# A down projection by seven products of 2x2 blocks, and the last modulation columns in the up loop

## The chip, the cores and the metric

The kernel runs on one core of a Trainium2 chip. Five engines work side by side on a common on-chip memory of 128 partitions (SBUF): TensorE (PE in the profile; PEld is its load of the stationary operand), VectorE (DVE), ScalarE (ACT), GpSimd (POOL) and SyncE (SP), which here only issues DMAs. TensorE writes to PSUM, eight banks of 128 x 512 fp32. Each engine works through its own instructions in order and waits on semaphores for the others. The metric is the device time of one execution in microseconds, the median of several runs.

## The reference

One layer of a diffusion backbone, for a prompt of 128 tokens and a sample of 512, both of width 1024. What matters here is the second half of the layer, a ConvFFN with a gain `g2` that comes from a conditioning vector, and the norm at the end:

```python
mod = jax.nn.silu(cvec) @ lw['w_ada'] + lw['b_ada']
sh1, sc1, g1, sh2, sc2, g2 = jnp.split(mod, 6, axis=-1)
...
h = rmsnorm(x, lw['norm2_g']) * (1.0 + sc2) + sh2
x = x + g2 * conv_ffn(h, lw['w_up'], lw['ffn_conv_w'], lw['ffn_conv_b'], lw['w_down'])
...
def conv_ffn(h, w_up, cw, cb, w_down):
    z = dwconv3(h @ w_up, cw, cb)
    a, g = jnp.split(z, 2, axis=-1)
    return (jax.nn.silu(g) * a) @ w_down
...
y_sample = rmsnorm(xs, final_norm_g)
```

`w_up` is 1024 x 5632, `w_down` 2816 x 1024, all in fp32.

## The kernel before

The 640 tokens (four tiles of 128 of the sample, one of the prompt) go through the layer together. Every fp32 product is made of three matmuls on two-part operands: the high part is a rounded copy made by ACT (`act(..., AF.Copy)`), the low part the difference, made by DVE (`tensor_tensor(..., subtract)`); high x high, high x low and low x high are added up in PSUM.

**The up loop** (`up_all`, `up_pair`, lines 1503 to 1657) runs over 22 pairs of an a-tile and a g-tile of the 2816 hidden features. Each pair is a product of 2x2 blocks with seven multiplications (`prod`, 12 matmuls of 320 columns each) in place of eight. The order of every engine is written out by hand there: calls through `ovec`, `opool` and `oact` keep their program order while `fixed[0]` is set. In `up_pair(p_)` TensorE works on pair p_ and on the last two products of pair q = p_ - 1; DVE makes the low parts and block sums of the weights of pair n = p_ + 1 (`up_al`, `up_sums`, `up_bl`), moves products out of PSUM (`first_sum` and the subtractions into `ubuf`), and runs the three-tap convolution of the pairs q and o = p_ - 2 (`taps`, two instructions of 128x641) and the gate (`gated`); ACT makes high parts, copies products and does `centre` and `gate`. POOL issues DMAs: two that make low parts by adding in memory (`low_dma`), and `keep`, which writes the finished 128x641 tile of activations to `actd` in DRAM. The tiles X1 (`xz`), X0 and MG1 (`ubuf`) hold the loop's intermediates, G half of the raw weights, F the block sums.

**The down stage** (`down_prep`, `down_tile`, `down_out`, lines 1695 to 1779) runs over two halves of the 1024 output columns and, in each, over 11 pairs of hidden tiles. A unit is one pair in one half: five token tiles x two hidden tiles x three matmuls of 512 columns with the activations stationary. Its operands are prepared two units ahead: 128x1024 of weights, and two activation tiles of 128x640 that are read back from `actd` in groups. The last three units of the second half are held, and their matmuls run token tile by token tile, each followed by its output steps. Tile's scheduler chooses the order within an engine here, by program order and readiness. Beside it `ada_cols` (lines 231 to 270) computes the columns 40 to 47 of the modulation, which are `g2`: a load of 128x1024 of `w_ada`, and for each of the two conditioning vectors one DVE instruction that multiplies and sums along the row. The finished columns are transposed on TensorE and go through DRAM (`gain_rows`) to be broadcast to all partitions (`gain_load`, into S0). The residual stream `x2` comes back from DRAM to X0, X1 and G (`x2r`) during the stage.

DMAs of weights are issued by SP, in program order: one that waits for its target to come free holds back those behind it. The tiles with tags `w`, `raw` and `gt` have 3, 3 and 4 buffers, those made by `region` one each.

## Time and profile before

| what | value |
|---|---|
| median of 3 runs | 1036.48 us (1036.42 to 1037.4) |
| the profiled execution | 1039.72 us, its span 1038.0 us, granted clock 0.994 |
| up loop, pairs 4 to 21 | 12.32 us a pair |
| last matmul of the up loop | 884.4 us after the span's start |
| down stage, a unit of 30 matmuls | 6.80 us |

An execution's own time is a little longer than its span in the trace, and the profiled one is a little longer than the median; times read in the trace are microseconds from the span's start. In rows of the trace `out<-in` names the tiles that an instruction writes and reads, `x12` is a count, a bracket tells how long the engine was idle before and what it waited for, and L146 is the line of the helper that records the hand-ordered calls, so there the tiles tell the instructions apart.

### The profile page before, as it was taken

How to read it: one execution, taken by the hardware profiler on the slowest of the kernel's cores; microseconds unless marked ns; L12 is line 12 of the kernel's file. 1: busy time of each engine (PE TensorE's matmuls, PEld its weight loads, DVE VectorE, ACT ScalarE, POOL GpSimd, SP SyncE). 2: the span in 40 equal slices, each digit the busy share in tenths (PEclk: the TensorE clock that was granted, in tenths of full speed). 3: DMA queues.
4: the chain of work that ended last, by engine and by line, in shares of the span. 5: the costliest groups of instructions: out<-in, count | busy, mean ns of one | idle time of the engine just before them, and what ended most of it. 6: DMA issues, size and time to landing. Idle time of an engine off the chain costs nothing.

```text
span 1038.0 us, 18800 instructions
## 1 busy us (share of the span) xinstructions
PE 1022.1 (98%) x7644; PEld 963.4 (93%) x7644; DVE 790.9 (76%) x1287; ACT 523.4 (50%) x905; POOL 95.8 (9%) x139
## 2 busy tenths in 40 slices
PE   8999999999999999999999999999999999999997
PEld 6899989998999999999998889999999999888886
DVE  6758889789956567767768689998888887795734
ACT  6642343342333444444445377876677776632532
POOL 1000010201100000000000021211111121000201
PEclk9999989999999999999999999999999999999998
DMA  9864433454144132332268385666655569974212
GB/s 355 317 212 131 126 96 122 131 179 152 52 141 140 52 102 81 124 102 77 66 229 328 132 260 144 173 168 166 163 149 151 148 152 260 373 250 156 82 41 102
DMA packets 54295, 165.68 MB, mean 160 GB/s; under 512 B 7968, under 2 KB 14912, under 8 KB 52160
## 3 DMA queue, kind: packets, MB, share of 16 engines
q1 hardware_dynamic: 44432, 137.19, 39.1%
q0 software_dynamic: 9776, 27.28, 11.3%
q8 instruction: 60, 0.98, 0.4%
q14 instruction: 27, 0.22, 0.1%
HBM read 131.52 MB, written 21.52 MB: 147 GB/s over the span
## 4 chain that ended last, share of the span: by engine, by line
PE 96%; DMA 2%; DVE 1%; issue 1%; ACT 0%; SPq 0%; POOL 0%; POOLq 0%
PE g L352 20%; PE g L1430 20%; PE m L1089 14%; PE g L1745 8%; PE m L1745 6%; PE m L1430 5%; PE g L1102 4%; PE m L1225 3%; PE g L901 2%; PE g L1225 2%; PE m L146 2%; PE g L146 1%; PE m L513 1%; DMA A<-in_w_ada_dram 1%; PE m L838 1%; PE m L801 1%
## 5 line engine op out<-in xcount | busy, mean ns | idle before, releaser
L352 PE MATMUL g<-XH,w 128*128 128x320 f32 x832 | 201.1, 319 | 0.0
L352 PEld LDWEIGHTS g<-XH,w 128*128 128x128 f32 x832 | 143.7, 191 | 2.0 <-issue 1.2
L352 PE MATMUL g<-XL,w 128*128 128x320 f32 x416 | 130.0, 312 | 0.0
L352 PEld LDWEIGHTS g<-XL,w 128*128 128x128 f32 x416 | 79.3, 191 | 0.3 <-issue 0.2
L304 DVE TENSOR_TENSOR w<-raw,w 128x1024 fp32r<-128x1024 f32 x34 | 41.6, 1222 | 18.8 <-ACT w L303 18.1
L1745 PE MATMUL g<-w,XH 128*128 128x512 f32 (+1 forms) x216 | 47.5, 372 | 0.0
L303 ACT ACTIVATE w<-raw 128x1024 fp32r<-128x1024 f32 x34 | 35.8, 1052 | 21.1 <-PE g L1225 10.2
L1745 PEld LDWEIGHTS g<-w,XH 128*128 128x128 f32 x216 | 38.5, 188 | 7.5 <-ACT XH L1708 0.3
L1089 PE MATMUL m<-XH,w 128*128 128x320 f32 x192 | 45.0, 309 | 0.0
L146 DVE SCALAR_TENSOR_TENSOR X<-MG,p2t,X 128x641 f32<-128x641 f32 x44 | 38.9, 885 | 5.7 <-ACT X L146 4.8
L316 ACT ACTIVATE w<-raw 128x1024 fp32r<-128x1024 f32 (+1 forms) x26 | 29.4, 1130 | 24.7 <-PE g L352 11.9
L146 DVE SCALAR_TENSOR_TENSOR X<-X,p2t,X 128x641 f32<-128x641 f32 x44 | 38.9, 885 | 2.0 <-ACT X L146 1.0
L1745 PE MATMUL m<-w,XH 128*128 128x512 f32 (+1 forms) x180 | 40.2, 368 | 0.0
L1745 PE MATMUL g<-w,XL 128*128 128x512 f32 (+1 forms) x180 | 40.1, 373 | 0.0
L1430 PE MATMUL g<-XL,C 128*128 128x320 f32 x240 | 38.6, 310 | 0.4 <-ACT MG L146 0.4
L1430 PE MATMUL g<-XL,w 128*128 128x320 f32 x240 | 38.7, 310 | 0.0
L317 DVE TENSOR_TENSOR w<-raw,w 128x1024 fp32r<-128x1024 f32 (+1 forms) x26 | 33.9, 1304 | 6.1 <-ACT w L316 5.8
L1745 PEld LDWEIGHTS g<-w,XL 128*128 128x128 f32 x180 | 32.2, 188 | 6.8 <-DVE dt L1756 0.6
L1430 PEld LDWEIGHTS g<-XL,C 128*128 128x128 f32 x240 | 35.9, 188 | 1.1 <-ACT MG L146 1.1
L1430 PEld LDWEIGHTS g<-XL,w 128*128 128x128 f32 x240 | 35.9, 188 | 0.5 <-ACT MG L146 0.3
L1745 PEld LDWEIGHTS m<-w,XH 128*128 128x128 f32 x180 | 31.3, 189 | 5.3
L1745 PE MATMUL m<-w,XL 128*128 128x512 f32 (+1 forms) x150 | 33.2, 368 | 0.0
(542 smaller groups left out, 2705.3 us busy)
## 6 DMA issues: line engine op xcount, KB each, us to landing
raw<-in_w_up_dram SPq DMA_DIRECT2D x31, 512.0 KB, 5.0
raw<-in_w_gp_dram SPq DMA_DIRECT2D x18, 640.0 KB, 3.9
raw<-in_w_down_dram SPq DMA_DIRECT2D x22, 512.0 KB, 3.9
raw<-in_w_in_dram SPq DMA_DIRECT2D x19, 512.0 KB, 4.5
H<-in_w_adt_dram SPq DMA_DIRECT2D x16, 512.0 KB, 4.3
actd<-X POOLq DMA_DIRECT2D x22, 320.5 KB, 5.4
G<-in_w_up_dram SPq DMA_DIRECT2D x11, 512.0 KB, 4.6
X<-in_w_adt_dram SPq DMA_DIRECT2D x10, 512.0 KB, 4.0
```

The source lines that it names most:

```text
L146: r = f(*args, **kw)
L303: act(w[0], raw, AF.Copy)
L304: vec.tensor_tensor(w[1], raw, w[0].bitcast(F32), ALU.subtract)
L316: high = lambda: act(w[:, 0], raw, AF.Copy)
L317: low = lambda: vec.tensor_tensor(w[:, 1], raw, w[:, 0].bitcast(F32), ALU.subtract)
L352: mm(o, w[:, h, k0 + k, :], r(k)[:, s], start=(k == 0 and i == 0), stop=(k == kt - 1 and i == 2))
L901: mm(o, x(kx)[:, ts], w[:, h, k, :], start=(kx == 0 and i == 0), stop=(kx == 7 and i == 2))
L1089: mm(o, w[:, k, :], x[:, k, :], start=(first and k == 0 and j == 0), stop=(k == 3 and j == 2), skip_group_check=True)
L1102: mm(pb[:, c, 0:HC], w[:, h + k, :], y[:, x, k, s], start=(k == 0 and j == 0), stop=(k == 1 and j == 2))
L1225: mm(m, mh[k // 2][:, hx, k % 2, t * P:(t + 1) * P], wo[q][:, hw, k % 2, :], start=(k == 0 and i == 0), stop=(k == 7 and i == 2))
L1430: mm(o, w[:, k, :], x[:, k, :], start=(first and k == 0 and j == 0), stop=(k == 3 and j == 2), skip_group_check=True)
L1745: mm(acc[nh][t + c0 // 256][:, 0:c1 - c0], sl[k][hx][:, t * P:(t + 1) * P], w[:, hw, k, c0:c1], start=(kk_ == 0 and k == 0 and i == 0), st ...
```

## The change

The down projection is done in 11 steps, one for each pair of hidden tiles, and twice over (`dn_first` and `dn_second`). For the 512 tokens of the sample a step is a product of 2x2 blocks: two token halves of 256, two hidden tiles, two column halves of 512. Seven products stand for eight: in the first pass the products 1, 6, 5 and 7, in the second 2, 3 and 4, and the prompt's tile, which is done plainly. The sums of weight blocks that this takes are three 128x512 instructions on POOL in each step (`dn_prep` with "T"), those of activation blocks are DVE's ("S"), and the splits into high and low parts ACT's and DVE's ("A", "B"). One activation block of each step is kept from the first pass for the second (`dn_keep`). Between the passes and in the second one, products 1, 5, 6 and 7 are combined and added to the residual (`dn_rest`, `dn_add`). The last three steps of the second pass are held and worked off output by output (`HOLD`). The order of all engines is now written out by hand.

The columns 40 to 47 of the modulation move into the up loop: in pairs 3 to 18 a load of 128x1024 (each column tile is loaded twice, once for each vector), a product on POOL (`ada_prod`) and, one pair later, a sum on ACT by a copy with an accumulator (`ada_sum`). The last round of `up_pair`, with only the end of pair 21, becomes `up_end`, in which the first steps of the down stage are mixed; the last taps and gates run in its first steps (`dlate`).

```diff
@@ -1520,6 +1520,35 @@
+    ADA = 3
+    dl, dn, dlate = {}, {}, {}
+    arl = const.tile([P, 2, 8], F32, name="arl")
+    def ada_sum(p_):
+        i = p_ - ADA
+        if i == -1:
+            cr = fx["cr"] = region("S0", [P, 2, D])
+            cf = cr.rearrange("p v c -> p (v c)")
+            nc.sync.dma_start(cf, a["cc"].rearrange("v c -> (v c)").partition_broadcast(P))
+        if i == 0:
+            cf = fx["cr"].rearrange("p v c -> p (v c)")
+            oact(cf, cf, AF.Silu)
+        if 0 < i <= 16:
+            oact(fx["ah"], fx["ah"], AF.Copy, accum_out=arl[:, (i - 1) % 2, (i - 1) // 2:(i - 1) // 2 + 1])
+        if 0 <= i < 16:
+            fx["ah"] = region("H", [P, D])
+            nc.sync.dma_start(fx["ah"], a["w_adt"][24 + i // 2])
+        if i == 17:
+            for v in range(2):
+                ovec.tensor_tensor(gcol[:, 1, v], arl[:, v], p1[:, C_BADA + 40:C_BADA + 48], ALU.add)
+            gain_rows(1)
+    def ada_prod(p_):
+        i = p_ - ADA
+        if 0 <= i < 16:
+            opool.tensor_tensor(fx["ah"], fx["ah"], fx["cr"][:, i % 2], ALU.mult)
...
@@ -1541,6 +1570,7 @@
         if nx and n >= BRIDGE:
             up_ah(n, r[n][0])
             up_al(n, r[n][0])
+        ada_sum(p_)
         if inner and p_ >= BRIDGE:
             up_start(p_)
             first_sum(p_)
@@ -1551,18 +1581,22 @@
             up_sums(n, r[n], 0)
             up_sums(n, r[n], 1)
         elif p_ == NPAIR - 1:
-            rd[UP + 1] = units[UP + 1][1](ld[UP + 1])
+            dl[1] = dn_load(0, 1)
+            dn_prep(0, 0, dl[0], "T")
         if inner and p_:
             up_c(p_, r[p_])
         if o >= 0:
             keep(o)
+        ada_prod(p_)
+        if p_ == NPAIR - 1:
+            dn_prep(0, 0, dl[0], "AS")
+            dn_prep(0, 1, dl[1], "T")
+            dl[2] = dn_load(0, 2)
         if inner:
             if p_ + 2 < NPAIR:
                 r[p_ + 2] = up_load(p_ + 2)
             elif p_ + 2 == NPAIR:
-                fx["a01"] = rp.tile([P, 2, T], F32, tag="raw", name=nm("raw"))
-                back(fx["a01"], 0, 2)
-                ld[UP + 1] = units[UP + 1][0]()
+                dl[0] = dn_load(0, 0)
         if q >= 0:
 
             c1 = up[q, "b"][0]
@@ -1586,10 +1620,41 @@
             centre(q, 1)
         if nx:
             up_bl(n)
+        else:
+            dn_prep(0, 0, dl[0], "B")
         if inner:
             b1, b2 = up[p_, "b"]
             prod(b2, p_, 5, True)
             prod(b1, p_, 7, False)
+    def up_end():
+        q = NPAIR - 1
+        c1, c2_ = up[q, "b"]
+        oact(tmp(2), c1, AF.Copy)
+        for (i0, i1, c) in S2:
+            ovec.tensor_tensor(ubuf(q, 1)[:, c:c + i1 - i0], c2_[:, i0:i1], tmp(2)[:, i0:i1], ALU.subtract)
+        dl[3] = dn_load(0, 3)
+        dn_m1(0, dn[0])
+        dn_prep(0, 1, dl[1], "AS")
+        dn_prep(0, 2, dl[2], "T")
+        prod(c1, q, 4, False)
+        for (i0, i1, c) in S2:
+            oact(ubuf(q, 0)[:, c:c + i1 - i0], c1[:, i0:i1], AF.Copy)
+        dn_m1(1, dn[1])
+        dn_prep(0, 1, dl[1], "B")
+        prod(c2_, q, 3, False)
+        ovec.tensor_tensor(ubuf(q, 1)[:, 1:1 + HC], c2_, tmp(q % 2), ALU.subtract)
+        dn_rest(0, dn[0])
+        dn_prep(0, 2, dl[2], "AS")
+        dn_m1(2, dn[2])
+        dn_prep(0, 2, dl[2], "B")
+        dlate[0] = lambda: taps(q - 1, 1)
+        dlate[1] = lambda: (gate(q - 1), gated(q - 1), keep(q - 1), centre(q, 0))
+        dlate[2] = lambda: (taps(q, 0), centre(q, 1))
+        dlate[3] = lambda: taps(q, 1)
+        dlate[4] = lambda: (gate(q), gated(q), keep(q))
...
-        for p_ in range(NPAIR + 1):
+        for p_ in range(NPAIR):
             up_pair(p_, r)
+        up_end()
...
-        start(ada_cols(range(40, 48), "MG1", lambda f: region("H", [P, D]) if f % 2 else down_home(), 5))
...
+    def dn_load(ps_, s_):
+        i = ps_ * NS + s_
+        if i < 3 or i % 4 == 2:
+            r = region(("MG0", "E", "F")[i] if i < 3 else "MG1", [P, 5, 512])
+        else:
+            r = wp.tile([P, 5, 512], F32, tag="w", name=nm("w"))
+        x = rp.tile([P, 5, 256], F32, tag="raw", name=nm("raw"))
+        if ps_ == 0:
+            nc.sync.dma_start(r[:, 0:3], a["w_dn1"][s_])
+            nc.sync.dma_start(x[:, 0:2], actd[2 * s_][:, 0:TS].rearrange("p (h t) -> p h t", h=2))
+            nc.sync.dma_start(x[:, 2], actd[2 * s_ + 1][:, 256:TS])
+        else:
+            nc.sync.dma_start(r[:, 0:4], a["w_dn2"][s_])
+            nc.sync.dma_start(x[:, 0:2], actd[2 * s_ + 1][:, 0:TS].rearrange("p (h t) -> p h t", h=2))
+            for j in range(2):
+                nc.sync.dma_start(x[:, 2, j * P:(j + 1) * P], actd[2 * s_ + j][:, TS + 1:T + 1])
+        return r, x
...
+    def dn_prep(ps_, s_, ld_, parts):
+        r, x = ld_
+        i = ps_ * NS + s_
+        n = i % 3
+        tt = ovec.tensor_tensor
+        def split(h, l, v):
+            oact(h, v, AF.Copy)
+            tt(l, v, h.bitcast(F32), ALU.subtract)
+        if "T" in parts:
+            if ps_ == 0:
+                opool.tensor_tensor(r[:, 2], r[:, 2], r[:, 1], ALU.subtract)
+                opool.tensor_tensor(r[:, 1], r[:, 1], r[:, 0], ALU.subtract)
+                opool.tensor_tensor(r[:, 3], r[:, 2], r[:, 0], ALU.add)
+            else:
+                opool.tensor_tensor(r[:, 4], r[:, 2], r[:, 0], ALU.subtract)
+                opool.tensor_tensor(r[:, 4], r[:, 4], r[:, 3], ALU.add)
+                opool.tensor_tensor(r[:, 4], r[:, 4], r[:, 1], ALU.subtract)
+            return
+        if i not in dn and parts != "S":
+            if n == 0:
+                w = region("XH", [P, 2, 5, 512], F32R)
+                wh, wl = w[:, 0], w[:, 1]
+            else:
+                wh, wl = [region(t, [P, 5, 512], F32R) for t in (("A", "B"), ("XL0", "XL1"))[n - 1]]
+            if i:
+                xx = region("ECD"[n], [P, 2, 4, 256], F32R)
+            else:
+                xx = wp.tile([P, 2, 4, 256], F32R, tag="w", name=nm("xx"))
+            dn[i] = (wh, wl), (xx[:, 0], xx[:, 1])
+        (wh, wl), (xh_, xl_) = dn.get(i) or ((None, None), (None, None))
+        if ps_ == 1 and "S" in parts:
+            tt(x[:, 3], x[:, 0], dn_keep(s_), ALU.subtract)
+        if ps_ == 1 and "B" in parts:
+            split(wh[:, 0:4], wl[:, 0:4], r[:, 0:4])
+            split(xh_, xl_, x[:, 0:4])
+            split(wh[:, 4], wl[:, 4], r[:, 4])
+        if ps_ == 1:
+            return
+        if "S" in parts:
+            tt(x[:, 3], x[:, 1], x[:, 2], ALU.add)
+            tt(x[:, 1], x[:, 0], x[:, 1], ALU.subtract)
+            tt(x[:, 2], x[:, 2], x[:, 1], ALU.subtract)
+        c0, c1 = 0 if "A" in parts else 1, 4 if "B" in parts else 1
+        if c0 < c1:
+            split(xh_[:, c0:c1], xl_[:, c0:c1], x[:, c0:c1])
+            split(wh[:, c0:c1], wl[:, c0:c1], r[:, c0:c1])
+        if "B" in parts:
+            oact(dn_keep(s_), x[:, 2], AF.Copy)
+    def dn_mm(o, st, wi, xi, c0, first=False, stop=False, cs=(0, 512)):
+        w, x = st
+        for i, (hx, hw) in enumerate(((0, 0), (0, 1), (1, 0))):
+            mm(o[:, cs[0]:cs[1]], x[hx][:, xi, c0:c0 + P], w[hw][:, wi, cs[0]:cs[1]],
+               start=(first and i == 0), stop=(stop and i == 2), skip_group_check=True)
...
+    def dn_m1(s_, st):
+        for t in range(2):
+            dn_mm(bank(1)[t], st, 0, 0, t * P, s_ == 0, s_ == NS - 1)
+    def dn_rest(s_, st):
+        last = s_ == NS - 1
+        if last:
+            u2 = dn["u2"] = dn["f"][:, D:2 * D].rearrange("p (a b) -> p a b", a=2)
+            oact(u2, dn["g1"], AF.Copy)
+        for m, wi, xi in ((6, 3, 2), (5, 1, 3), (7, 2, 1)):
+            for t in range(2):
+                dn_mm(bank(m)[t], st, wi, xi, t * P, s_ == 0, last)
...
+    def dn_first(s_, st):
+        if s_ == 4:
+            f = dn["f"] = region("F", [P, 2560])
+            nc.sync.dma_start(f[:, 0:D], a["final_norm_g"].partition_broadcast(P))
+            grows["g2"] = gain_load(1, "S0")
             x2[0:2] = [x2r("X0")[:, 0:1024], x2r("X0")[:, 1024:2048]]
+            x2[2:4] = [x2r("X1")[:, 0:1024], x2r("X1")[:, 1024:2048]]
             x2[4] = x2r("G")[:, 0:1024]
+        if s_ > 2:
+            dn_m1(s_, st)
+        if s_:
+            dn_rest(s_, st)
+    def dn_add(k):
+        u2, g = dn["u2"], grows["g2"]
+        t = k % 2
+        if k < 2:
+            x = dn["x57"][t]
+            ovec.tensor_tensor(x, x, u2[:, t], ALU.add)
+            opool.tensor_tensor(x, x, g[:, 0, 512:], ALU.mult)
+            c = x2[2 + t][:, 512:]
+            ovec.tensor_tensor(c, c, x, ALU.add)
+            dn_half(2 + t, 512, 1024, x)
+            return
+        n = (k - 2) // 2
+        cs = slice(n * 512, n * 512 + 512)
+        c = x2[t if n else 2 + t][:, cs]
+        v = gp.tile([P, 512], F32, tag="gt", name=nm("dv"))
+        opool.tensor_tensor(v, u2[:, t], g[:, 0, cs], ALU.mult)
+        ovec.tensor_tensor(c, c, v, ALU.add)
+    def dn_half(t, c0, c1, junk):
+        xs, q = x2[t][:, c0:c1], st3[:, t:t + 1]
+        oact(junk, xs, AF.Square, accum_out=q)
+        opool.tensor_tensor(xs, xs, dn["f"][:, c0:c1], ALU.mult)
...
+    HOLD = 3
+    def dn_second(s_, st):
+        b = dn["b"]
+        if s_ == 0:
+            b["p"] = [pm(), pm()]
+        end = s_ >= NS - HOLD
+        def prod(m, sts, t, cs=(0, 512), o=None, first=False):
+            wi, xi = {2: (2, 0), 3: (0, 3), 4: (4, 1)}[m]
+            for x in sts:
+                dn_mm(o or b[{2: 1, 3: 5, 4: 7}[m]][t], x, wi, xi, t * P, first and x is sts[0],
+                      end and x is sts[-1], cs)
+        def prompt(sts, n):
+            for x in sts:
+                for j in range(2):
+                    dn_mm(b["p"][n], x, ((1, 2), (3, 0))[n][j], 2, j * P, s_ == 0 and j == 0,
...
+        if not end:
+            for m in (2, "p", 3, 4):
+                for t in range(2):
+                    if m == "p":
+                        prompt([st], t)
+                    else:
+                        prod(m, [st], t)
+            if 0 < s_ < 7:
+                dn_add(s_ - 1)
+            return
+        h = dn.setdefault("hold", [])
+        h.append(st)
+        if s_ < NS - 1:
+            return
+
+        dn_plus(1, 1, b[5][1][:, 256:512], 256, 512)
...
+    def dn_all(_):
+        fixed[0] = True
+        sd = [(ps_, s_) for ps_ in range(2) for s_ in range(NS)]
+        for i, (ps_, s_) in enumerate(sd):
+            if i + 4 < 2 * NS:
+                dl[i + 4] = dn_load(*sd[i + 4])
+            if i + 3 < 2 * NS:
+                dn_prep(*sd[i + 3], dl[i + 3], "T")
+                dn_prep(*sd[i + 3], dl[i + 3], "S")
+            if 2 < i + 2 < 2 * NS:
+                dn_prep(*sd[i + 2], dl[i + 2], "AB")
+            if i in dlate:
+                dlate[i]()
+            if i == 2 * NS - 1:
+                fixed[0] = False
+            (dn_second if ps_ else dn_first)(s_, dn[i])
...
+    b11, b12, b21, b22 = w[:, 0, :, 0], w[:, 0, :, 1], w[:, 1, :, 0], w[:, 1, :, 1]
+    arr["w_dn1"] = np.ascontiguousarray(np.stack([b11, b12, b22], 2))
+    arr["w_dn2"] = np.ascontiguousarray(np.stack([b22, b11, b21, b12], 2))
```

`w_dn1` and `w_dn2` hold the blocks of `w_down` that the passes load, 128x1536 and 128x2048 for a step, laid out on the host.

183 lines of the change are left out of this document (71 added, 112 removed).

## The prediction

> **What bounds the kernel now.** I read the page first (its head, and the chain that ended last), then the busy time of each engine in windows of the two stages that the change touches, then the pieces of the chain.
>
> ```profile
> span 1038.0 us, 18800 instructions
> PE 1022.1 (98%) x7644; PEld 963.4 (93%) x7644; DVE 790.9 (76%) x1287; ACT 523.4 (50%) x905; POOL 95.8 (9%) x139
> PE 96%; DMA 2%; DVE 1%; issue 1%; ACT 0%; SPq 0%; POOL 0%; POOLq 0%
> ```
>
> ```profile
> core 0: us, PE busy (x) PEld busy (x) DVE busy (x) ACT busy (x) POOL busy (x), PEclk, DMA share, GB/s
> 758.64:770.96 12.32, 12.32 (x86) 12.32 (x85) 10.92 (x17) 8.80 (x16) 2.18 (x4) 1.00 0.61 153
> 884.36:1009.32 124.96, 124.96 (x594) 104.50 (x593) 85.88 (x119) 51.92 (x73) 8.29 (x6) 1.00 0.53 181
> ```
>
> ```profile
> 780.42 10.56 PE g L1430 x72
> 790.98 1.76 PE m L1430 x12
> ```
>
> ```profile
> 900.04 5.44 PE g L1745 x24
> 905.48 1.36 PE m L1745 x6
> ```
>
> TensorE is the bound, at full clock, in both stages. An up pair is 84 matmuls of 320 columns in 12.32 us (0.1467 us each); a down unit is 30 matmuls of 512 in 6.80 us (0.2267 us each). The first window is one up pair: DVE is busy 10.92 of 12.32, so only 1.40 us of it are free. The second is the down stage: DVE is at 69%, POOL almost unused.
>
> **What the change removes.** Before, a pair of ff tiles costs 2 halves x 30 = 60 matmuls. After, it costs 7 products x 2 tiles x 3 = 42 for the sample and 2 tiles x 2 halves x 3 = 12 for the prompt: 54. Over 11 steps 594 stand for 660, and 66 x 0.2267 = 15.0 us of TensorE go. In the first pass a step is 24 matmuls (5.44 us), in the second 30 (6.80). The 16 reductions of the last modulation columns leave DVE in the down stage, where they were hidden, so this saves nothing by itself. If TensorE stayed the bound, that would be all: 1036.5 - 15.0 = 1021.5.
>
> **What it adds on POOL, and the price to DVE.** Sixteen 128x1024 products in pairs 3 to 18, three 128x512 sums for each of the 22 steps, and eight 128x512 products in `dn_add`. The trace has places where such POOL instructions ran beside DVE:
>
> ```profile
> 958.81 1.29 POOL L1763 TENSOR_TENSOR X<-X,F 128x512 f32<-128x512 f32 x1 [65.24 <-ACT dt L1762]
> 961.89 2.55 POOL L1763 TENSOR_TENSOR X<-X,F 128x512 f32<-128x512 f32 x2 [1.79 <-ACT dt L1762]
> 965.83 2.06 POOL L1763 TENSOR_TENSOR X<-X,F 128x512 f32<-128x512 f32 x1 [1.39 <-ACT dt L1762]
> 967.85 1.89 POOL L1763 TENSOR_TENSOR G<-G,F 128x512 f32<-128x512 f32 x1
> ```
>
> ```profile
> 962.97 0.68 DVE L1756 TENSOR_TENSOR dt<-m,S 128x512 f32<-128x512 f32 x1
> ...
> 965.51 1.21 DVE L304 TENSOR_TENSOR w<-raw,w 128x1024 fp32r<-128x1024 f32 x1
> 966.65 0.14 DVE L1764 TENSOR_SCALAR st<-st 128x1 f32<-128x1 f32 x1
> 966.71 1.85 DVE L1711 TENSOR_TENSOR XL<-C,XL 128x640 fp32r<-128x640 f32 x1
> ...
> 968.55 1.86 DVE L1711 TENSOR_TENSOR XL<-C,XL 128x640 fp32r<-128x640 f32 x1
> ```
>
> ```profile
> L1711 DVE TENSOR_TENSOR XH<-A,XH x6: 814/818/826, 899.7 to 978.0; 128x640 fp32r<-128x640 f32 x6
> ```
>
> Alone, POOL's 128x512 takes 1.29 us and DVE's 128x640 takes 0.82. Meeting, DVE's took 1.85 and 1.86, 1.03 longer each, and POOL's took 2.06 and 1.89. They go strictly in turn: POOL waited until DVE's 1024 was through (965.51 + 1.21 = 966.72; 2.06 - 1.29 after 965.83 is 966.60), then DVE stood until POOL was. So one 128x512 on POOL costs DVE 1.03 us when DVE has an instruction with both operands in SBUF. The 962.97 row, whose operand m is in PSUM, fell inside a POOL instruction (961.89 to 964.44) and took its usual 0.68: such instructions are free of it.
>
> The Trainium skill states this as a rule: its page "SBUF — State Buffer", section "Who interferes with whom", says that a DVE instruction with two SBUF inputs contends with a GpSimd instruction that reads SBUF, and that one of the two blocks fully for the whole of the other. The rows above agree (1.85 beside 0.82). By this rule nearly every DVE instruction of both stages is exposed; without it the sum would be the 1021.5 above.
>
> For 128x1024 the trace has no row. A smaller one gives the slope:
>
> ```profile
> L793 POOL TENSOR_TENSOR B<-X x16: 732/742/1987, 200.3 to 283.7; 128x256 f32<-128x256 f32 x16
> ```
>
> ```profile
> 200.35 2.03 DVE L617 TENSOR_TENSOR MG<-MG,hss 128x1280 f32<-128x1280 f32 x1 [3.65 <-POOL hss L298]
> ```
>
> ```profile
> L317 DVE TENSOR_TENSOR w<-raw,w 128x1280 fp32r<-128x1280 f32 x8 | 11.9, 1486 | 0.5 <-ACT w L316 0.4
> ```
>
> ```profile
> H<-in_w_adt_dram SPq DMA_DIRECT2D x16, 512.0 KB, 4.3
> ```
>
> A 128x256 (0.74 us alone) cost DVE 2.03 - 1.49 = 0.54, a 128x512 1.03: 0.49 more for 256 elements, so 1024 costs about 2.0. Its bounds are 0.6, where it falls on all the time in which DVE waits (1.40), and 2.4, POOL's own length (1.29 + 2 x 0.55). I take 2.0: the load of H lands 4.3 us after its issue, and POOL then meets the block sums and taps, all SBUF with SBUF.
>
> **Up loop.** The prices alone, of DVE and of ACT:
>
> ```profile
> L304 DVE TENSOR_TENSOR w<-raw,w 128x1024 fp32r<-128x1024 f32 x34 | 41.6, 1222 | 18.8 <-ACT w L303 18.1
> L303 ACT ACTIVATE w<-raw 128x1024 fp32r<-128x1024 f32 x34 | 35.8, 1052 | 21.1 <-PE g L1225 10.2
> L146 DVE SCALAR_TENSOR_TENSOR X<-MG,p2t,X 128x641 f32<-128x641 f32 x44 | 38.9, 885 | 5.7 <-ACT X L146 4.8
> L146 DVE TENSOR_TENSOR F<-F,raw 128x512 f32<-128x512 f32 x31 | 21.3, 687 | 0.3
> ```
>
> What is late next, and from when, is in these rows (the bracket is the wait before an instruction):
>
> ```profile
> 659.53 0.49 DVE L146 TENSOR_TENSOR MG<-m,s 128x320 f32<-128x320 f32 x1
> ...
> 852.28 1.23 DVE L146 TENSOR_TENSOR w<-raw,w 128x1024 fp32r<-128x1024 f32 x1 [0.35 <-ACT w L146]
> 854.45 0.49 DVE L146 TENSOR_TENSOR MG<-m,s 128x320 f32<-128x320 f32 x1 [0.95 <-PE m L1430]
> ...
> 859.84 0.48 DVE L146 TENSOR_TENSOR X<-g,X 128x320 f32<-128x320 f32 x1
> 861.98 1.81 DVE L146 SCALAR_TENSOR_TENSOR X<-X,p2t,X 128x641 f32<-128x641 f32 x2
> 863.70 0.55 DVE L146 TENSOR_TENSOR X<-g,X 128x192 f32<-128x192 f32 x2
> ```
>
> ```profile
> 655.30 1.92 PE L1430 MATMUL m<-XH,MG 128*128 128x320 f32 x12
> ...
> 862.98 1.92 PE L1430 MATMUL g<-XH,w 128*128 128x320 f32 x12
> ```
>
> DVE's X<-g,X (ends 860.32) gives back the PSUM bank that product 1 of the next pair fills at 862.98: DVE may be 2.7 us late before TensorE stands. At pair 4 it is late already: its MG<-m,s starts 2.3 us after product 2 ends (657.2), without a wait. A pair with a POOL product costs DVE 10.92 + 2.0 = 12.9, 0.6 over TensorE. Pair 3 adds 2.0, pairs 4 to 18 add 15 x 0.6 = 9.0: 2.3 + 2.0 + 9.0 - 2.7 = 10.6, say 11 us of TensorE late (bounds 0 and 16, from the prices 0.6 and 2.4). Pairs 19 and 20 have no product, and DVE makes up its 2.7.
>
> ACT's added sum of 128x1024 (some 1.1, by the row of ACT) makes 8.80 into 9.9 of 12.9: covered by ACT's waits; without cover it would be 1.1 a pair. The 16 loads of 0.5 MB stand in front of the weight loads on SP and wait for that sum; the DMA share, 0.61, leaves room. POOL, 2.18 busy in the window, has room for 2.4 more. The transpose of the finished gain columns can cost TensorE one wait in pair 20, for DVE's additions behind w<-raw,w (852.28 + 1.23, against product 1's start 12.32 before 862.98): 2.9 us, and TensorE is owed more than that by the down stage, so I add nothing.
>
> **Down stage.** By the rows of prices above, each DVE instruction starting 0.07 before the one ahead ends (966.65 against 966.72), 1024 elements take 1.15, 512 take 0.62, and at that slope 256 take 0.35 and 2048 2.21. A first-pass step: 3 x 0.35 + 1.15 (tokens) + 2.21 (weights) = 4.41. A second-pass step: 0.35 + 1.15 + 2.21 + 0.62 = 4.33. POOL adds 3 x 1.03 = 3.09 to both. So DVE and POOL in turn need 7.5 and 7.4 us where TensorE needs 5.44 and 6.80: the three sums must cost DVE under 0.34 each in the first pass for TensorE to stay the bound.
>
> The ledger of DVE from the start of pair 21 to the last split:
> - 11 x 4.41 + 11 x 4.33 + 66 x 1.03 = 164.1;
> - pair 21's own work without next weights: two taps 2 x 1.72 (861.98 to 863.70), subtractions 0.47 and 0.41, sum 0.41, gate 0.73: 5.4; `up_end` 0.9; the late taps and gates 3 x 1.72 + 2 x 0.73 = 6.6;
> - the sums at the end of the first pass 4 x 0.62 = 2.5; `dn_add`: 8 POOL products of 1.03 and 5.1 of DVE, 13.3.
>
> Together 193. Each step's matmuls wait for its splits, made two steps ahead, and these for POOL's sums; with no reserve left TensorE starves, and its saved 15 us are idle time. ACT's share of a step, 3.2 to 3.8 us at 1.05 per 1024, stays covered. Then the held 90 matmuls of the last three steps: 20.4, less 1.4 that need only the first two, 19.0.
>
> ```profile
> 1029.16 1.60 PE L1745 MATMUL m<-w,XH 128*128 128x256 f32 x12
> ```
>
> After its last matmul (1030.8) the kernel before takes 7.2 us to its end, and the new end is the same kind of chain.
>
> DVE starts pair 21 at 862.0 + 11 = 873; + 193 = 1066; + 19 + 7.2 = 1092 of span, against 1038.0. Two corrections: PSUM operands in the ledger (some 3.5 us) can run beside POOL, -3; and the queue below, +4.
>
> ```profile
> L146 POOL DMA_DIRECT2D actd<-X x22 | 19.0, 866 | 19.6 <-DVE X L146 19.6
> ```
>
> ```profile
> actd<-X POOLq DMA_DIRECT2D x22, 320.5 KB, 5.4
> X<-x2d SPq DMA_DIRECT2D x4, 512.0 KB, 7.1
> ```
>
> At step 4 SP is given the reload of X1, which waits until the last act tile has left X1 (issue 0.9 on POOL, 5.4 to land), and every later step's loads stand behind it. Loads of step 9 then land about 0.9 + 5.4 + 7.1 + 5 = 18 us after step 4's share of DVE, and are wanted after 7.5: a stall between 0 (the gate done early, and the reload fast) and 11; I take 4. All step loads together (11 x 1.1 MB and 11 x 1.4 MB, in 77 DMAs) are 28 MB in some 190 us, under the 181 GB/s of the window above.
>
> Net +55. The profiled execution took 1039.7 (1.7 beside its span), 3.2 over the median, so the sum on its own time is 1095, and on the median of the runs **1092**.
>
> **The rivals.**
> - *POOL gives way* (other side). If POOL used only DVE's gaps, TensorE would stay the bound from the point at which a 128x512 costs DVE under 0.34: 1021.5. For it: 1.40 us a pair and about 1 us a first-pass step are free. Against: 1.03, measured twice. Chance 0.11.
> - *The up loop absorbs its products.* If they fall on DVE's waits, the 11 us go: 1081. For it: 1.40 us of waits and 1.3 of PSUM operands in each pair. Against: landing times. 0.16.
> - *Half price.* At 0.6 per 128x512 and 1.2 per 1024, the loop pays nothing, and the ledger falls by 74 x 0.43 = 32: 1092 - 11 - 32 = 1049. Nothing in the rows is near it. 0.05.
> - *The queue at step 4* costs all 11: 1099. For it: the keep and the reload are in one chain. Against: step 9's weights have a buffer of their own. 0.08.
> - *The saving is not there* (matmuls wait as they do now, nothing contends): about 1036. 0.02.
>
> **How the numbers follow.** My forecast, DVE and POOL in turn in both stages, has 0.58; its own range is 1076 to 1106. The time is its sum, 1092. The range goes down to half price, 1050, and up to the upper bounds together (loop 16, queue 11, no overlap): 1092 + 5 + 7 + 3, rounded to 1108. Below 1050 lie POOL giving way, the missing saving and a little of half price, above 1108 a few hundredths. No change is what lies within 0.2% (2 us), about what a measurement of this kernel can tell: 0.03, of the last two rivals. Faster 0.11. Slower 0.86.
>
> **What would show it.** DVE instructions of 128x512 to 128x2048 in the down stage with means 1 us above the 0.69 and 1.22 of now, and POOL's 128x512 at 1.8 to 2.5 rather than 1.29; TensorE idle in front of L1745's successors, released by DVE; pair period 12.9 in place of 12.32 from pair 4; down stage some 45 us longer in spite of 66 matmuls less. I am wrong if DVE's durations stay as they are, or if the pair period stays 12.32 while POOL's products run.

## The result and the profile after

The changed kernel takes 1123.88 us (median of 4 runs, 1121.81 to 1125.75) and the kernel before 1036.45 on the same chip: a ratio of 1.084, with a 95% interval of 1.0826 to 1.0853. It is slower, as forecast, but 16 us beyond the top of the range and 32 us over the forecast. The profiled execution took 1122.25 us, its span 1120.4.

The page of the changed kernel, its head and the chain that ended last (which could be followed back over the last 17% of the span only), then windows of one up pair and of the down stage:

```profile
span 1120.4 us, 18807 instructions
PE 1032.7 (92%) x7521; PEld 956.1 (85%) x7521; DVE 928.9 (83%) x1298; ACT 560.2 (50%) x946; POOL 269.4 (24%) x227
...
DVE 10%; issue 3%; POOL 2%; DMA 1%; PE 1%; ACT 0%; SPq 0%; POOLq 0%; DVEq 0%; ACTq 0%
```

```profile
core 0: us, PE busy (x) PEld busy (x) DVE busy (x) ACT busy (x) POOL busy (x), PEclk, DMA share, GB/s
826.03:839.78 13.75, 12.82 (x86) 12.32 (x85) 13.64 (x17) 9.60 (x18) 4.73 (x4) 1.00 0.64 179
900.00:1092.30 192.30, 142.84 (x560) 111.43 (x560) 180.05 (x129) 80.26 (x85) 127.59 (x72) 0.89 0.48 156
```

The chain is DVE's now. In an up pair DVE is busy 13.64 of 13.75 us (before: 10.92 of 12.32), in the down stage 180.05 of 192.30; TensorE has idle time in both. The timelines of DVE and of POOL in one pair show why (start, duration, engine, line, operation):

```profile
704.23 0.69 DVE L146 TENSOR_TENSOR F<-F,raw 128x512 f32<-128x512 f32 x1
704.84 3.61 DVE L146 TENSOR_TENSOR F<-raw 128x512 f32<-128x512 f32 x1
```

```profile
704.56 0.88 POOL L146 DMA_DIRECT2D actd<-X  x1
705.15 2.74 POOL L146 TENSOR_TENSOR H<-H,S 128x1024 f32<-128x1024 f32 x1
```

One DVE instruction in a pair takes 3.61 in place of 0.69 (3.60 to 3.80 in fourteen of the pairs 4 to 18, 3.02 in one): the column product costs DVE 2.92, not the forecast 2.0, and DVE stands from before POOL's recorded start until POOL's end at 707.89. Pairs follow each other in 13.76 us, not 12.9 (DVE's move of product 2 starts at 674.62 in pair 5 and at 867.31 in pair 19, fourteen pairs later).

In the down stage the price is close to the forecast one: POOL's sums take 1.91 us in the mean, and DVE's 128x1024 and 128x2048 split take 1.08 and 1.07 more than the 1.22 and 2.28 that they need alone (timeline of DVE, and groups of POOL):

```profile
975.58 2.30 DVE L146 TENSOR_TENSOR D<-raw,D 128x1024 fp32r<-128x1024 f32 x1
977.80 3.35 DVE L146 TENSOR_TENSOR XL<-w,XL 128x2048 fp32r<-128x2048 f32 x1
```

```profile
L146 POOL TENSOR_TENSOR w<-w 128x512 f32<-128x512 f32 x45 | 85.6, 1909 | 15.4 <-DMA w<-in_w_dn_dram 13.5
```

The longest waits in the down stage, 890 to 1093, of DVE and then of TensorE (total, times, longest; L1820 is the line of the down stage's matmuls):

```profile
DVE X L146 <- POOL x L146: 2.8, 2, 1.4
DVE XL L146 <- ACT XL L146: 2.2, 2, 1.7
DVE xx L146 <- ACT xx L146: 2.0, 2, 1.7
DVE st L146 <- ACT x L146: 1.6, 2, 0.8
DVE X L146 <- POOL dv L146: 1.2, 1, 1.2
DVE X L146 <- PE g L1430: 1.2, 1, 1.2
```

```profile
PE g L1820 <- DVE B L146: 14.3, 4, 5.1
PE g L1820 <- DVE XL L146: 10.7, 3, 4.9
PE m L1820 <- DVE F L146: 7.4, 1, 7.4
PE g L1820 <- DVE XH L146: 7.3, 3, 3.6
```

TensorE waits for DVE's splits, and DVE itself waits some 12 us for ACT, POOL and TensorE, which the ledger of the prediction had at nothing.

**The miss as a sum.** The prediction's span was 1093 (1092 on the median by adding 1.7 and taking off 3.2). Measured against it: DVE begins pair 21 at 890.88 with 3.1 of its ledger (the first three sums) already behind it, 14.8 later than 873; from there to the end of the last split at 1092.3 it needs 204.5 with those 3.1, 10.5 more than 193 - 3 + 4; from the split to the end 28.1 in place of 26.2. Together 27.2, and 1093 + 27.2 = 1120.2. The other 4.8 us are the step from one execution to the median: the profiled execution of before lay 3.2 above its median, that of the changed kernel 1.6 below.

### The profile page after: what moved, and what is told of

Read it like the earlier page. It is cut to its first block, busy times and chain, and to the rows that moved or that the text cites. A ratio compares the mean times of both kernels' runs of the same rounds, so it can differ in the third digit from the quotient of the medians.

```text
span 1120.4 us, 18807 instructions
## 1 busy us (share of the span) xinstructions
PE 1032.7 (92%) x7521; PEld 956.1 (85%) x7521; DVE 928.9 (83%) x1298; ACT 560.2 (50%) x946; POOL 269.4 (24%) x227
## 5 line engine op out<-in xcount | busy, mean ns | idle before, releaser
L146 POOL TENSOR_TENSOR w<-w 128x512 f32<-128x512 f32 x45 | 85.6, 1909 | 15.4 <-DMA w<-in_w_dn_dram 13.5
L146 DVE SCALAR_TENSOR_TENSOR X<-MG,p2t,X 128x641 f32<-128x641 f32 x44 | 44.0, 1000 | 3.0 <-ACT X L146 2.0
L146 POOL TENSOR_TENSOR H<-H,S 128x1024 f32<-128x1024 f32 x16 | 44.0, 2748 | 0.0
L146 ACT ACTIVATE X<-X,p2t 128x641 f32<-128x641 f32 x22 | 20.4, 927 | 44.4 <-DVE X L146 44.4
L1820 PE MATMUL g<-XL,D 128*128 128x512 f32 (+1 forms) x87 | 27.1, 430 | 13.1 <-DVE XL L146 10.7
L1820 PE MATMUL m<-XL,D 128*128 128x512 f32 (+1 forms) x108 | 30.8, 434 | 7.4 <-DVE F L146 7.4
L146 ACT ACTIVATE w<-F 128x512 fp32r<-128x512 f32 (+1 forms) x44 | 30.6, 729 | 13.3 <-DVE F L146 13.2
L146 ACT ACTIVATE C<-raw 128x512 fp32r<-128x512 f32 (+3 forms) x40 | 27.1, 716 | 16.9 <-DVE raw L146 10.3
L1820 PE MATMUL g<-XH,E 128*128 128x512 f32 (+1 forms) x87 | 24.9, 408 | 11.4 <-DVE XH L146 7.3
L1820 PEld LDWEIGHTS m<-XL,D 128*128 128x128 f32 x108 | 23.6, 221 | 13.4 <-DVE F L146 7.9
```

The lines of the kernel that those rows point to most:

```text
L146: r = f(*args, **kw)
L1820: mm(o[:, cs[0]:cs[1]], x[hx][:, xi, c0:c0 + P], w[hw][:, wi, cs[0]:cs[1]], start=(first and i == 0), stop=(stop and i == 2), skip_group_c ...
```

## The experiments

Each variant was executed once, beside one execution of the kernel before on the same chip, which took between 1035.9 and 1038.5. The changed kernel's own runs lie 4 us apart, so less than that is not read as a difference of the totals; the rows of the traces carry the rest. "Product 1" is TensorE's first product of pair 21: 862.98 before, 887.99 in the changed kernel.

**POOL writes, but does not read.** The column product becomes three memsets of H; `g2` is left out.

```diff
-            opool.tensor_tensor(fx["ah"], fx["ah"], fx["cr"][:, i % 2], ALU.mult)
+            for _ in range(3):
+                opool.memset(fx["ah"], 0.0)
```

> The changed kernel with each of POOL's 16 products in the up loop replaced by three memsets of the same 128x1024 tile (some 2.8 us of POOL, which only write); g2 is left out, ACT's sums and the loads stay. Theory, turns on SBUF reads: DVE's instruction in the middle of each pair falls from 3.0 to 3.6 us back to 0.69, the pair period from 13.8 to 12.3, pair 21 starts some 24 us earlier, time 1097 to 1103. Rival, any POOL work of that length or the moved loads and sums slow the loop: period stays 13.5 or more, time 1118 to 1126.

Measured: 1094.18, 3 under the range of the theory. POOL is as busy as before the edit, at the same place behind the keep, and DVE does not notice (timelines of POOL and of DVE):

```profile
705.83 0.80 POOL L146 DMA_DIRECT2D actd<-X  x1
706.39 3.23 POOL L146 MEMSET H<- 128x1024 f32 x3
```

```profile
706.12 0.69 DVE L146 TENSOR_TENSOR F<-F,raw 128x512 f32<-128x512 f32 x1
706.72 1.80 DVE L146 SCALAR_TENSOR_TENSOR X<-MG,p2t,X 128x641 f32<-128x641 f32 x2
...
715.37 0.49 DVE L146 TENSOR_TENSOR MG<-m,s 128x320 f32<-128x320 f32 x1 [0.95 <-PE m L1430]
```

DVE's 0.69 and 1.80 are those of the kernel before, it waits for TensorE again, and a pair takes 12.32 (its move of product 2 starts at 703.05 and at 715.37). The DMA issue costs DVE nothing by itself: the instruction from 706.12 runs beside the issue (705.83 to 706.63) and keeps its 0.69. It is POOL's reading that costs DVE. The rule of the Trainium skill ("SBUF — State Buffer", "Who interferes with whom") says just this, that a POOL instruction which only writes does not contend; these rows agree. 30 us hang on it.

**The sums left out.** The 66 block sums are not computed; a loaded block stands in for the last sum of each step.

```diff
             nc.sync.dma_start(r[:, 0:3], a["w_dn1"][s_])
+            nc.sync.dma_start(r[:, 3], a["w_dn2"][s_][:, 0])
...
             nc.sync.dma_start(r[:, 0:4], a["w_dn2"][s_])
+            nc.sync.dma_start(r[:, 4], a["w_dn1"][s_][:, 0])
...
+        if "T" in parts:
+            return
```

> The changed kernel with POOL's 66 sums of weight blocks left out; a block from DRAM stands in the place of each last sum, so DVE, ACT and TensorE do the same work on other numbers, and the loads grow by 256 KB a step. Theory, turns: DVE's 128x2048 falls to 2.28 throughout, TensorE is the bound again in the down stage, the time from pair 21 to the end falls from 232 us to 158 to 170: 1045 to 1060. Rival, the loads or ACT's splits hold the down stage: over 1090.

Measured: 1066.61, above the range. All the splits of 128x2048 but one are back at 2.28 to 2.29 (the one, 3.12 at 1005.89, meets a product of `dn_add`, which POOL still makes), so the sums are what made them longer, but the rest is not TensorE's alone: product 1 starts at 888.55, 25.6 late, and 1066.6 - 25.6 = 1041 is still not below the kernel before. DVE is nearly full without POOL, and now a load comes late (windows with the columns of those above, then DVE's timeline):

```profile
910.00:930.00 20.00, 19.14 (x84) 15.33 (x83) 19.27 (x26) 14.09 (x16) 0.57 (x1) 1.00 0.80 278
950.00:970.00 20.00, 15.39 (x59) 12.21 (x58) 13.25 (x13) 8.72 (x9) 0.00 (x0) 0.83 0.91 335
```

```profile
958.97 1.34 DVE L146 TENSOR_TENSOR raw<-raw 128x256 f32<-128x256 f32 x3 [6.68 <-DMA raw<-actd]
```

The activations stood behind the reload of X1 in SP's queue, which the prediction had at +4: it is there, at 6.7 (with 0.25 MB a step more to load than in the changed kernel, which has its share in it), but only where DVE is early. In the changed kernel no instruction of DVE waits for a load in the down stage; POOL's sums do (13.5 us in the group shown above, 8.2 the longest), while DVE has other work.

**The columns on DVE**, as one multiply-accumulate a pair; POOL and ACT have nothing to do with them.

```diff
-            oact(fx["ah"], fx["ah"], AF.Copy, accum_out=arl[:, (i - 1) % 2, (i - 1) // 2:(i - 1) // 2 + 1])
+            ovec.scalar_tensor_tensor(fx["ah"], fx["ah"], 1.0, fx["cr"][:, (i - 1) % 2], ALU.mult, ALU.mult,
+                                      accum_out=arl[:, (i - 1) % 2, (i - 1) // 2:(i - 1) // 2 + 1])
...
-            opool.tensor_tensor(fx["ah"], fx["ah"], fx["cr"][:, i % 2], ALU.mult)
```

> The changed kernel with the product on POOL and the sum on ACT replaced by one multiply-and-sum on DVE in each of pairs 3 to 18 (1.15 us more DVE work than the changed kernel has of its own). Theory, turns cost 2.9 and the work itself costs 1.15: a pair is 10.92 + 1.2 = 12.1 of DVE, period 12.32 again, time 1097 to 1105. Rival, DVE is simply full and any more work on it makes the loop slower than with POOL: 1124 to 1140.

Measured: 1096.06, 1 under the range of the theory, product 1 at 863.22. The group of the new instruction, and the window of one pair, in which TensorE has no idle time again:

```profile
L146 DVE SCALAR_TENSOR_TENSOR H<-H,S 128x1024 f32<-128x1024 f32 x16 | 19.5, 1219 | 0.0
```

```profile
758.64:770.96 12.32, 12.32 (x86) 12.32 (x86) 12.21 (x19) 8.78 (x17) 2.32 (x4) 1.00 0.76 211
```

Doing the work itself costs DVE 1.22 a pair, and fits; having POOL make the product alone costs it 2.92, and does not.

**The sums on DVE.** The first of the six lines of "T"; the others alike.

```diff
-                opool.tensor_tensor(r[:, 2], r[:, 2], r[:, 1], ALU.subtract)
+                ovec.tensor_tensor(r[:, 2], r[:, 2], r[:, 1], ALU.subtract)
```

> The changed kernel with the 66 sums of 128x512 made by DVE in place of POOL. Theory, turns: a sum costs DVE 0.62 of its own in place of 1.08 of standing still, 66 x 0.46 = 30 us less, time 1090 to 1100. Rival, POOL's sums cost DVE little and something else is slow: DVE gets 41 us more, time 1140 to 1165.

Measured: 1103.57, 20 less than the changed kernel. Three sums take DVE 2.01 where POOL's cost it 3 x 1.08. It misses the range by 3.6, with new waits of DVE for loads:

```profile
DVE MG L146 <- DMA MG<-in_w_dn_dram: 6.4, 1, 6.4
DVE E L146 <- DMA E<-in_w_dn_dram: 4.3, 1, 4.3
```

**Both on DVE**: the edits of the last two together.

> The column products (one multiply-accumulate a pair) and all 66 weight-block sums are DVE's; only the eight products of dn_add and the norm's stay on POOL. My theory: the two prices were paid at different places and in the same currency, DVE's time, so the two gains add up: 1124 - 28 (columns alone) - 20 (sums alone) = 1076, range 1068 to 1084; the last pair's product 1 near 863, and TensorE still waits for DVE in the first pass, where DVE's step is 4.41 + 3 x 0.65 = 6.4 us against 5.44. Rival: the up loop's lateness was partly hidden behind the down stage's slow start, so the gains don't add up: 1088 to 1096. Rival: without any POOL beside DVE the saved 66 matmuls come through: 1020 to 1035.

Measured: 1078.34. The gains add up (27.8 + 20.3 off 1123.88 is 1075.8): the two prices are paid one behind the other, in DVE's time.

**The up loop's part alone**: the kernel before, with the columns moved as in the change. `ada_sum` and `ada_prod` are added and called as there; the old reductions go.

```diff
-        start(ada_cols(range(40, 48), "MG1", lambda f: region("H", [P, D]) if f % 2 else down_home(), 5))
...
-            drain(lambda: "ada47" in R)
```

> The kernel before with the columns moved into the up loop as the change has it (product on POOL, sum on ACT) and the down stage as before; DVE's sixteen reductions beside the down stage are gone. My theory: the whole cost is the up loop's lateness, as in the changed kernel: product 1 of the last pair some 25 us later than the 862.98 of before, the down stage as long as before, 1059 to 1066 in all. By the price that my prediction took (2.0 a product) it would be 11 us: 1047 to 1050. Rival: the lateness comes from what the change puts into pairs 20 and 21 and from its loads, not from the products: under 1043.

Measured: 1067.06, a touch over the range and far from the 1047 to 1050 of the prediction's price. Product 1 starts at 890.59, 27.6 late, and the span is 1065.3, 27.3 over that of before. TensorE's lateness in the loop passes to the end one for one.

**The product in two halves**, straight behind each other.

```diff
-            opool.tensor_tensor(fx["ah"], fx["ah"], fx["cr"][:, i % 2], ALU.mult)
+            for c0 in (0, 512):
+                opool.tensor_tensor(fx["ah"][:, c0:c0 + 512], fx["ah"][:, c0:c0 + 512],
+                                    fx["cr"][:, i % 2, c0:c0 + 512], ALU.mult)
```

> The changed kernel with each column product on POOL cut into two instructions of 128x512. If DVE's price goes by the 512-element instruction measured in the down stage (1.03 to 1.08 each), a pair costs DVE 2.1 instead of 2.9: pair period 12.9 to 13.1 in place of 13.8, 1109 to 1114. Rival: the price goes by the elements POOL reads, however they are cut: pair period 13.7 to 13.9, 1121 to 1127. Rival: between the halves DVE gets its turn and each half waits and blocks once more: 1127 or above.

Measured: 1127.65, a pair 13.94: the time of the last rival, but not its mechanism. DVE gets no turn between the halves; it stands for both, 3.74 in place of 0.69 (timelines of POOL and of DVE):

```profile
707.40 0.89 POOL L146 DMA_DIRECT2D actd<-X  x1
707.99 2.87 POOL L146 TENSOR_TENSOR H<-H,S 128x512 f32<-128x512 f32 x2
```

```profile
707.68 3.74 DVE L146 TENSOR_TENSOR F<-raw 128x512 f32<-128x512 f32 x1
```

These rows gave a new theory. The keep's issue ends at 707.40 + 0.89 = 708.29, and 2 x 1.29 later it is 710.87: just where the halves end (710.86). In the changed kernel 704.56 + 0.88 + 2.4 = 707.84, and the product ends at 707.89. So POOL takes up the product while its DMA issue still runs, DVE stands from then on, and pays for a piece of the issue too.

**The halves apart**, the first ahead of the pair's adding DMAs, the second behind the keep.

```diff
...
+        ada_prod(p_, 0)
         if inner and p_:
             up_c(p_, r[p_])
         if o >= 0:
             keep(o)
-        ada_prod(p_)
+        ada_prod(p_, 1)
```

> The changed kernel with each column product on POOL cut into two instructions of 128x512, the first ahead of the pair's adding DMAs and the second behind the keep, so that they lie apart. If DVE stands for the whole of a run of POOL instructions and a single 128x512 costs it the 1.03 to 1.08 of the down stage, a pair costs 2.1 and not 2.9 to 3.05: last pair's product 1 some 12 us earlier than the 887.99 of the changed kernel, 1109 to 1115 in all. Rival: the price in the up loop goes by POOL's own time per element (1.37 or more for 512) wherever the halves lie: 1120 to 1130.

Measured: 1131.07, so the total went the other way (a pair takes 14.2), but the timelines of POOL and of DVE tell two prices for one size:

```profile
708.65 1.57 POOL L146 TENSOR_TENSOR H<-H,S 128x512 f32<-128x512 f32 x1 [7.66 <-ACT X L146]
...
711.32 1.17 POOL L146 DMA_DIRECT2D actd<-X  x1
711.90 1.91 POOL L146 TENSOR_TENSOR H<-H,S 128x512 f32<-128x512 f32 x1
```

```profile
708.98 1.80 DVE L146 TENSOR_TENSOR F<-F,raw 128x512 f32<-128x512 f32 x1
710.70 3.81 DVE L146 SCALAR_TENSOR_TENSOR X<-MG,p2t,X 128x641 f32<-128x641 f32 x2
```

The half that POOL begins after a wait costs DVE 1.11 (1.80 for 0.69), as in the down stage; the one behind a DMA issue costs 2.01 (3.81 for 1.80), though both are 128x512. Neither of the stated theories had that: 1.11 + 2.01 = 3.1 is as dear as one piece.

**A later load** was to make the product start from a wait: the load of H is issued behind those of the raw weights.

```diff
     def ada_sum(p_):
...
-        if 0 <= i < 16:
-            fx["ah"] = region("H", [P, D])
-            nc.sync.dma_start(fx["ah"], a["w_adt"][24 + i // 2])
...
     def ada_prod(p_):
         i = p_ - ADA
         if 0 <= i < 16:
+            fx["ah"] = region("H", [P, D])
+            nc.sync.dma_start(fx["ah"], a["w_adt"][24 + i // 2])
             opool.tensor_tensor(fx["ah"], fx["ah"], fx["cr"][:, i % 2], ALU.mult)
```

with the call of `ada_prod` moved behind `up_load`.

> The changed kernel; only the load of w_ada (tile H) is issued later in the pair, behind the loads of the raw weights, so that POOL's product waits for that load and no longer follows straight on the issue of the keep's DMA. My theory: in the changed kernel POOL's product is taken up while that issue still runs (705.15 against 704.56 + 0.88 = 705.44), and DVE stands from then on: 0.3 us of the issue, 2.4 of the product and some 0.2, 2.92 in all. A product that POOL begins from idleness waits for DVE's running instruction and costs DVE its own 2.39 less 0.2 (as 1.29 costs 1.08 in the down stage): 2.1 to 2.3. Pair period 13.0 to 13.2 in place of 13.8, last pair's product 1 near 877 in place of 888, 1109 to 1115; POOL's 128x1024 recorded at 2.4 plus what it waits for DVE. Rival: the product costs 2.9 wherever it begins: 1120 to 1127.

Measured: 1124.46. The edit missed its aim: H still came free and landed early enough, POOL began at 705.72 behind an issue from 705.13 for 0.89, and DVE's instruction took 3.61. It says nothing about the theory.

**The whole product ahead of the adding DMAs.**

```diff
+        ada_prod(p_)
         if inner and p_:
             up_c(p_, r[p_])
         if o >= 0:
             keep(o)
-        ada_prod(p_)
```

> The changed kernel with POOL's column product of 128x1024 whole, but ahead of the pair's two adding DMAs and the keep instead of straight behind them; POOL then waits for the load or for ACT's sum and begins it from idleness. With the halves laid apart, the half that began so cost DVE 1.11 (1.80 in place of 0.69) and the half behind the keep 2.01 (3.81 in place of 1.80). My theory: DVE stands from about 0.2 us before POOL's recorded start, and behind a DMA issue that start lies in the issue, so 0.3 to 0.6 of it and the wait for the turn are paid too. Ahead of the DMAs the product costs DVE 2.39 - 0.2 = 2.1 to 2.3 in place of 2.9: last pair's product 1 near 877 in place of 888, 1109 to 1116. Rival: a 128x1024 costs 2.9 wherever it begins: 1121 to 1127. Rival: the adding DMAs, now behind the product, come late for TensorE: above 1127.

Measured: 1131.44. The price falls as the theory has it, the total does not. DVE's instructions that meet the product take 3.03 for 1.21, 2.90 for 0.69 and 3.84 for 1.80, that is 1.8 to 2.2 more. The second of them is a block sum, the kind that took 3.61 in the changed kernel, so the lower price is not that of another DVE instruction (POOL, then DVE):

```profile
719.93 2.91 POOL L146 TENSOR_TENSOR H<-H,S 128x1024 f32<-128x1024 f32 x1 [7.85 <-DMA H<-in_w_adt_dram]
```

```profile
720.49 2.90 DVE L146 TENSOR_TENSOR F<-F,raw 128x512 f32<-128x512 f32 x1
```

But the adding DMA that reads G is now issued behind the product, so G's reload is late, and from 655 to 855 DVE waits 14.1 us for it:

```profile
DVE F L146 <- DMA G<-in_w_up_dram: 14.1, 6, 4.8
```

**ACT's sum later**, which keeps H longer, so that its load lands when POOL is idle and the order of POOL's DMAs stays. On top of the later load:

```diff
     def ada_sum(p_):
...
-        if 0 < i <= 16:
-            oact(fx["ah"], fx["ah"], AF.Copy, accum_out=arl[:, (i - 1) % 2, (i - 1) // 2:(i - 1) // 2 + 1])
...
     def ada_prod(p_):
         i = p_ - ADA
+        if 0 < i <= 16:
+            oact(fx["ah"], fx["ah"], AF.Copy, accum_out=arl[:, (i - 1) % 2, (i - 1) // 2:(i - 1) // 2 + 1])
```

> The changed kernel; ACT's sum of the finished product stands behind its copies for the pair's adding DMAs, so H comes free later, its load lands later, and POOL's product waits for that load some microseconds behind the keep's issue: it begins from idleness and the order of POOL's DMAs stays as it is. My theory: the product then costs DVE 2.0 to 2.2, as it did ahead of the adding DMAs (3.03 for 1.21, 2.90 for 0.69, 3.84 for 1.80), and not 2.9, and here nothing else comes late: DVE and TensorE period 13.0 to 13.2, last pair's product 1 near 877 in place of 888, 1109 to 1116. Rival: what the product saves is lost to a load again (DVE waits for raw weights): 1121 or above. Rival: the price is 2.9 also here: 1121 to 1127.

Measured: 1115.17, product 1 at 879.38. POOL's product, and in DVE's timeline the instruction that meets it, between three of its moves of product 2 (pairs 5, 19 and 20):

```profile
712.98 2.42 POOL L146 TENSOR_TENSOR H<-H,S 128x1024 f32<-128x1024 f32 x1 [6.57 <-DMA H<-in_w_adt_dram]
```

```profile
677.41 0.48 DVE L146 TENSOR_TENSOR MG<-m,s 128x320 f32<-128x320 f32 x1
...
713.16 3.31 DVE L146 TENSOR_TENSOR w<-raw,w 128x1024 fp32r<-128x1024 f32 x1
...
858.60 0.48 DVE L146 TENSOR_TENSOR MG<-m,s 128x320 f32<-128x320 f32 x1
872.03 0.49 DVE L146 TENSOR_TENSOR MG<-m,s 128x320 f32<-128x320 f32 x1 [2.21 <-PE m L1430]
```

Begun from idleness the product lasts 2.42 and costs DVE 2.1 (3.31 for 1.21; 1.75 to 2.2 in other pairs). Fourteen pairs take 858.60 - 677.41 = 181.19, 12.94 each: the period of the prediction. DVE waits for nothing in these pairs, here as in the changed kernel, so the same work on the same engine costs it 0.8 us more or less a pair by what POOL does just ahead of it.

**Relieving DVE.** On top of the kernel with both on DVE: some low parts by adding in memory, the products of `dn_add` on DVE, late taps a step earlier, the reloads of X1 and G two steps later. The core of the edit:

```diff
-            split(wh[:, 0:4], wl[:, 0:4], r[:, 0:4])
+            oact(wh[:, 0:4], r[:, 0:4], AF.Copy)
+            low_dma(wl[:, 2:4], r[:, 2:4])
+            tt(wl[:, 0:2], r[:, 0:2], wh[:, 0:2].bitcast(F32), ALU.subtract)
```

> On top of the kernel with columns and sums on DVE: DVE is relieved where the trace of that kernel shows it late. The low parts of one weight block in four (first pass) and of two in five (second pass) are made by adding in memory, as the up loop does; the products of dn_add are DVE's; the last taps and gates run one step earlier, so that MG1 comes free for step 6; the reloads of X1 and G go two steps later. My theory, that DVE's time and its waits for loads set the end of the down stage: 188 us of DVE from pair 21 to the last split, less 10 of waits for loads, 6 and 13 of low parts, 6 of the chains of dn_add and 6 of standing behind POOL, plus 5 of products, make 152; with the same tail of 25 the end is at 1042, the time 1038 to 1052. Rival: the added DMA traffic (0.25 MB and 0.5 MB a step, read and written) makes the loads late instead: 1060 or above. Rival: 66 matmuls less come through at last and the kernel is faster than before: under 1034.

Measured: 1064.67, the time of the first rival. Windows of it, with the same columns, and the two longest of TensorE's waits:

```profile
940.00:960.00 20.00, 17.62 (x70) 14.01 (x70) 19.54 (x26) 11.71 (x12) 2.99 (x4) 0.91 1.03 326
960.00:980.00 20.00, 15.82 (x62) 12.34 (x61) 16.15 (x24) 10.43 (x11) 1.72 (x2) 0.91 1.03 307
```

```profile
PE m L1826 <- DMA XH<-MG: 5.6, 2, 5.0
PE m L1826 <- DMA B<-w: 4.8, 2, 4.0
```

TensorE waits for the adding DMAs now, with the DMA engines full (share 1.03), while DVE has still 19.54 of 20 us to do in the first of the two windows. It is the fastest form of the changed kernel that was run, and 26 us slower than the kernel before. Whether another split of the low parts between DVE, ACT and DMA would bring the 15 us of TensorE through was not tried.

## Why the prediction was right in direction and wrong in size

1. *POOL and DVE in turn when both read SBUF*: right; the memsets (DVE's 0.69 unchanged) show it from the other side. Rivals that had POOL give way, at half price, or absorbed by the loop's 1.40 us of waits fall with it.
2. *1.03 for each 128x512 sum*: right (1.08 on the splits).
3. *2.0 for a 128x1024 product, "I take 2.0: the load of H lands 4.3 us after its issue, and POOL then meets the block sums and taps", with POOL's own length 2.4 as the upper bound*: this is the step that failed. The number holds for a product that POOL begins from a wait (2.1 and a pair of 12.94). In the change H had landed, and POOL was busy with its own queue: the product followed straight on the keep's DMA issue, cost 2.92, and the pair took 13.76. The prediction counted the instructions ahead of the product on POOL as busy time (2.18 of a pair) but did not ask what they do to DVE's turn, and so its bound was no bound. Over 16 pairs that is 16 x 0.86 = 13.8 of the 14.8 us. The 14.8 alone would have put the time at 1107, just within the range; the waits under 5, the tail under 7 and the 4.8 from one execution to the median took it out. (At the bound of 2.4 the working gives 2.3 + 2.4 + 15 x 1.0 - 2.7 = 17.0 of lateness, not the 16 that the prediction states.)
4. *The transposition of the gain columns at nothing, since TensorE is owed more*: wrong. The engine that sets the end is DVE, and DVE waited 2.24 us in pair 20 for the product behind the transposition; some 1.5 of it is the transposition's (product 1 is through at 875.28 + 1.76 = 877.04, product 2 starts at 878.52). The start of the loop was some 1 us better than put.
5. *The ledger of DVE*: its busy terms held (204.5 less 12.4 of waits is 192, for 193), its waits did not. It took DVE as never waiting; it waited 12.4 us, for ACT's copies and twice for the whole chain of `dn_add`, POOL's product and ACT's square (1.40 and 0.79). 204.5 against the plain 193 is 11.5, about these waits; whether the - 3 for PSUM operands came in can't be read apart.
6. *The queue at step 4, + 4*: not paid by DVE in the changed kernel, which was later than the loads; 6.7 where DVE was early, with more to load.
7. *The tail*: 28.1 for 26.2. The held matmuls went through in 17.8, 1.2 less than put; the end behind the last matmul (1110.1) took 10.3, not 7.2.
8. *15.0 us of TensorE*: the work is gone, the time is not. Even with the sums left out it is 176.3 us from product 1 to the end, against 175.0 before. DVE has 19.27 of 20 us to do in a window of the first pass there, one load is 6.7 late, and the end behind the last matmul takes 10.6 in place of 7.2; how the 15 us divide among these is not shown.

## What to carry to other kernels

Before work goes to an idle GpSimd, price it in VectorE's time: with both reading SBUF, VectorE stood for nearly the whole GpSimd instruction here (1.03 to 1.11 of 1.29 us), and where it could have done the work itself in less, the move is a loss. An upper bound for such a stall holds only if it covers what stands ahead of the instruction on GpSimd's own queue, here a DMA issue. And when the engine that sets the end changes, every wait of the new one has to be put in its ledger, not only its work.

## What was not expected of the hardware

A POOL instruction straight behind a DMA issue costs DVE more than one begun from a wait, as if it blocked DVE while the issue still runs: 2.92 against 2.1 for 128x1024, 2.01 against 1.11 for 128x512. That the turn is taken early is read from the ends of the instructions in three kernels; no run tried another kind of instruction ahead of it. Two independent POOL instructions straight behind each other held DVE for both (3.05 for two of 128x512).

TensorE slowed after a wait here. Its timeline in the changed kernel, matmuls of 512 columns:

```profile
943.79 0.50 PE L1820 MATMUL g<-B,C 128*128 128x512 f32 x1 [3.03 <-DVE B L146]
...
945.36 0.63 PE L1820 MATMUL m<-A,C 128*128 128x512 f32 x1
945.78 0.63 PE L1820 MATMUL m<-B,C 128*128 128x512 f32 x1
946.21 0.63 PE L1820 MATMUL m<-A,C 128*128 128x512 f32 x1
```

Starts lie 0.42 to 0.43 us apart in place of 0.2267. The granted clock is 0.52 from 945.06 to 948.34, so the slow stretch begins 1.3 us after the matmuls do; over the down stage it is 0.89. The Trainium skill describes it ("TensorE: Matmul & The Clock Gate", Part 1 on the clock gate): half rate for some 3.4 us after an idle stretch of about that length. The rows agree in the rate; the wait here was 3.03 and the slow stretch 3.3. That it set no time is argued, not shown: TensorE waits again soon after (2.01 us at 957.26). Its busy time is longer than before (1032.7 for 1022.1), with fewer matmuls.
